# Seven block products in place of eight in part of an MLP's second projection, with a fourth place for split weights

## The chip, the cores and the metric

The kernel runs on one core of a Trainium2 chip. A core has five engines with queues of their own: TensorE (PE) multiplies matrices, VectorE (DVE) and ScalarE (ACT) work elementwise, GpSimd (POOL) does a little here, and SyncE (SP) issues nearly all transfers (DMAs). Operands of the engines lie in an on-chip memory of 128 partitions; products accumulate in eight banks of PSUM, each 128 x 512 float32. The metric is the device time of one execution in microseconds, as the median of several runs.

## What is computed

The reference is one layer of a hybrid encoder over 256 tokens of 2048 features: a mixer with two branches, cross-attention, an MLP and a final norm. The change lies in the MLP:

```python
h = rms_norm(x, norm_ffn_g[l])
x = x + jnp.square(jax.nn.relu(h @ w_ff1[l])) @ w_ff2[l]
return rms_norm(x, norm_final_g)
```

`w_ff1` is 2048 x 8192 and `w_ff2` 8192 x 2048, float32. The hidden activations are 256 x 8192.

## The kernel before

**Split operands.** Each float32 operand of a large product is split into a high part (rounded to the type float32r) and a low part (the rest). A product is then three matmuls: high by high, high by low, low by high. For activations the pair is a *quad*, a tile of four 128-feature blocks by 256 tokens with both parts (`new_quad`); `quad_a` deals them from a ring of five. For weights, `fetch` loads a raw block of 1 MB (2048 float32 columns a partition, ring of three places, `raw`) by one DMA on SP's queue (L104), and splits it in two halves of 1024 columns each: ScalarE copies into `whi` (L117), VectorE subtracts into `wlo` (L118). `whi` and `wlo` have a ring of three places, so three halves can be held at a time. Loads and splits have a high priority in the scheduler, which gives the static order of each engine's queue by a planned time line. `latest` remembers the last split and load, `fetched` all loads; `tc.issue_after(ins)` queues what it encloses behind `ins` on that engine, without a wait.

**The MLP's loop.** The 8192 hidden features are worked off in four quarters, `fb` 0 to 3 (L1124 on). In each quarter:

- *First projection*: eight times `blocks`, each for 256 hidden features (one column pair): 16 feature blocks x 2 column blocks x 2 matmuls (L201 of 512 columns, high weights by both parts of the activations; L202 of 256 columns). `evac_h` (L1130) squares the positive part into `hs` and splits it into the quarter's four quads `hid` (L1134, L1135). In quarter 0, `place` moves 32 tokens at a time of the residual from `tr` to the token-major tile `res`.
- *Second projection*: four times `chunk`, for 512 output columns `n` each. A chunk goes through four stages `q` of 512 hidden features (one raw block each): 4 feature blocks x 2 token halves x 3 matmuls of 512 columns (L158, L159, L160). The two token halves accumulate in PSUM tiles `s0` and `s1`, two each (`stream_ps`); there are four more banks `b` (`bank`). At the end `add` (L1145) adds the scaled sum to `res` on VectorE. The last quarter also takes the sum of squares, and the last chunk (`evac_last`) ends the final norm.

The tiles `rt` and `tr` hold the residual by features and its transpose (16 KB a partition each); after the placement they aren't read any more. `gfin` holds the final gains, 8 KB a partition, loaded ahead of the MLP (L1109).

Of the kernel before, what the change touches and what calls it, by code (L numbers as in the profile page):

```python
# [10 lines left out]
F32 = mybir.dt.float32  # L11
F32R = mybir.dt.float32r
# [5 lines left out]
P = 128  # L18
# [34 lines left out]
def trunk(ctx: ExitStack, tc: tile.TileContext, x_f, mem_f, positions, lead_f, small_f, w_in, ret_gn_g, w_out, w_xq,  # L53
# [20 lines left out]


    fetched, steps, latest = [], [], {}

    @contextmanager
    def behind():
# [15 lines left out]
    def fetch(pieces, k, n, cuts=1, hold=None, at=(0, 0)):  # L95

        raw = wp.tile([P, k * n], F32, name="raw", tag="raw", bufs=3)
        rv = raw.rearrange("p (k n) -> p k n", k=k)
        with tc.high_priority(offset=100000):
            for off, ap in pieces:  # L100
                src = ap.rearrange("(k p) n -> p k n", p=P)
                for c in range(cuts):
                    ks = slice(c * k // cuts, (c + 1) * k // cuts)
                    fetched.append(nc.sync.dma_start(rv[:, ks, off:off + ap.shape[1]], src[:, ks, :]).ins)  # L104
            got = []
            for i in range(2):
                if hold:
                    both = hold().both
                    hi, lo = (both[:, a:a + 2, :].rearrange("p a s -> p (a s)") for a in (0, 2))
                else:  # L110
                    hi, lo = (wp.tile([P, k * n // 2 + room], F32R, name=nm, tag=nm, bufs=3)[:, a:a + k * n // 2]
                              for nm, a, room in zip(("whi", "wlo"), at, (64, 0)))
                src = raw[:, i * k * n // 2:(i + 1) * k * n // 2]
                part = k * n // max(cuts, 2)
                for c in range(0, k * n // 2, part):
                    cs = slice(c, c + part)
                    latest["hi"] = act.activation(hi[:, cs], src[:, cs], AF.Copy).ins  # L117
                    latest["lo"] = vec.tensor_sub(lo[:, cs], src[:, cs], hi[:, cs].bitcast(F32)).ins  # L118
                got.append((hi.rearrange("p (k n) -> p k n", n=n), lo.rearrange("p (k n) -> p k n", n=n)))
            latest["raw"] = fetched[-1]  # L120
        return got
# [23 lines left out]
    def chunk(quads, pieces_of, evac, before=None, hold=None, cuts=1):  # L145

        ps = stream_ps()
        parts = [(t, 0, 512, ps[t]) for t in range(NT)]
        if hold:
            parts[1:] = [(1, 0, 256, ps[1][:, :256]), (1, 256, 512, bank()[:, :256])]  # L150
        held = {q: fetch(pieces_of(q), 4, 512, hold=hold) for q in ((2, 3) if hold else ())}

        def products(q, i, part, halves):
            t, c0, c1, o = part
            xh, xl = (a[:, i, t * P:(t + 1) * P] for a in quads[q])
            wh, wl = (a[:, i % 2, c0:c1] for a in halves[i // 2])
            first, last = q == 0 and i == 0, q == 3 and i == 3
            pe.matmul(o, xh, wh, start=first, stop=False)  # L158
            pe.matmul(o, xh, wl, start=False, stop=False)  # L159
            pe.matmul(o, xl, wh, start=False, stop=last)  # L160

        for q in range(4):
            if q not in held:
                if before and q:
                    before(q)
                halves = fetch(pieces_of(q), 4, 512, cuts=1 if q else cuts)
                if before and not q:
                    before(q)
                for i in range(4):
                    for part in parts:  # L170
                        products(q, i, part, halves)
                    if i % 2:
                        step()
        for part in parts:
            for q, halves in held.items():
                for i in range(4):
                    products(q, i, part, halves)
            with tc.high_priority(offset=50000):
                evac(part[0], part[3], part[1], part[2])
# [93 lines left out]
    def square_sum(acc, src):  # L273
        junk = sm.tile([P, 512], F32, name="junk", tag="junk", bufs=1)
        act.activation(junk[:, :src.shape[1]], src, AF.Square, accum_out=acc)
# [829 lines left out]


    fp = ctx.enter_context(tc.tile_pool(name="mlp", bufs=2))
    gfin = fp.tile([P, D], F32, name="gfin", tag="gfin", bufs=1)
    nc.sync.dma_start(gfin, norm_final_g.partition_broadcast(P))  # L1109
    res = fp.tile([P, NT, D], F32, name="res", tag="res", bufs=1)  # L1110

    tr = fp.tile([P, KT, S], F32, name="tr", tag="tr", bufs=1)
# [3 lines left out]
    def place(b8):  # L1116

        with tc.issue_after(fetched[-1]):
            for a in range(4):
                to = res[b8 % 4 * 32:b8 % 4 * 32 + 32, b8 // 4, :].rearrange("i (k a f) -> i k a f", a=4, f=32)[:, :, a, :]  # L1120
                nc.sync.dma_start(to, tr[32 * a:32 * a + 32, :, b8 * 32:b8 * 32 + 32])

    ssq4 = cp.tile([P, NT, 5], F32, name="ssq4")
    for fb in range(4):  # L1124
        hid = []
        for b2 in range(8):
            hs = fp.tile([P, 2, S], F32, name="hs", tag="hs", bufs=2)
            if b2 % 2 == 0:
                hid.append(quad_a())

            def evac_h(b, ps):
                vec.scalar_tensor_tensor(hs[:, b, :], ps, 0.0, ps, op0=ALU.max, op1=ALU.mult)  # L1132
                qh, ql = (a[:, b2 % 2 * 2 + b, :] for a in hid[-1])
                act.activation(qh, hs[:, b, :], AF.Copy)  # L1134
                vec.tensor_sub(ql, hs[:, b, :], qh.bitcast(F32))  # L1135

            blocks(h3, w_ff1[0], fb * D + b2 * 256, 2, evac_h)
            if fb == 0:
                place(b2)
        for n in range(4):  # L1140
            ns = slice(n * 512, (n + 1) * 512)

            def add(t, ps, c0, c1):
                got = res[:, t, n * 512 + c0:n * 512 + c1]
                vec.scalar_tensor_tensor(got, ps, rstd3q[:, t:t + 1], got, op0=ALU.mult, op1=ALU.add)  # L1145
                return got

            def evac_o(t, ps, c0, c1):
                got = add(t, ps, 0, 512)
                if fb == 3:  # L1150
                    square_sum(ssq4[:, t, n:n + 1], got)
                    vec.tensor_mul(got, got, gfin[:, ns])

            def evac_last(t, ps, c0, c1):
                got = add(t, ps, c0, c1)
                acc = ssq4[:, t, 4 if c0 else 3:5 if c0 else 4]
                if t == 0:
                    square_sum(acc, got)
                else:
                    junk = sm.tile([P, 512], F32, name="junk", tag="junk", bufs=1)  # L1160
                    vec.scalar_tensor_tensor(junk[:, :256], got, 1.0, got, op0=ALU.mult, op1=ALU.mult, accum_out=acc)
                if not c0:
                    s = sm.tile([P, 1], F32, name="s4", tag="s4")
                    vec.tensor_reduce(s, ssq4[:, t, 0:4], axis=AX.X, op=ALU.add)
                    vec.tensor_scalar(s, s, 1.0 / D, EPS, op0=ALU.mult, op1=ALU.add)
                    sums.append(s)
                else:
                    vec.scalar_tensor_tensor(sums[t], acc, 1.0 / D, sums[t], op0=ALU.mult, op1=ALU.add)
                if c1 < 512:
                    return  # L1170
                r = sm.tile([P, 1], F32, name="r4", tag="r4")
                rsqrt(r, sums[t])
                if t == 0:
                    vec.tensor_mul(res[:, t, ns], res[:, t, ns], gfin[:, ns])
                for c in (0, 3, 1, 2):
                    cs = slice(c * 512, (c + 1) * 512)
                    o = res[:, t, cs]
                    if t and c == 3:
                        vec.scalar_tensor_tensor(o, o, r, gfin[:, cs], op0=ALU.mult, op1=ALU.mult)
                    elif t and c == 2:  # L1180
                        vec.tensor_scalar(o, o, r, None, op0=ALU.mult)
                    else:
                        act.activation(o, o, AF.Copy, scale=r)
                    (act if t and c in (3, 2) else nc.sync).dma_start(out[0, t * P:(t + 1) * P, cs], o)

            last = fb == 3 and n == 3
            sums = []
            chunk(hid, cols(w_ff2[0, fb * D:(fb + 1) * D, :], n * 512), evac_last if last else evac_o,
                  hold=quad_b if last else None)


_INS = ["positions", "w_in", "ret_gn_g", "w_out", "w_xq", "w_xkv", "w_xo", "w_ff1", "w_ff2", "norm_final_g"]
# [39 lines left out]
```

## Time and profile before

| what | us |
|---|---|
| median of three runs | 2066.09 (2065.47 to 2066.57) |
| the profiled execution | 2067.12 |
| its span, first to last instruction | 2065.4 |
| TensorE busy | 2055.6 |
| VectorE busy | 1413.0 |
| ScalarE busy | 1097.3 |
| GpSimd busy | 37.4 |

The profile is one execution. Each engine's busy time is the union of its instructions; a matmul's own duration overlaps with the next matmul's, so a pace is read from windows between two events. A group line gives line, engine, operation, tiles, shapes and count, then busy time and mean ns of one, then the idle time before them and what ended it. In timeline rows stand start, duration, engine, line and tiles, and in brackets the idle time before it with its releaser. A row of waits gives who waited for whom: total, times and longest.

### The profile page before, as it was taken

How to read it: one execution, taken by the hardware profiler on the slowest of the kernel's cores; microseconds unless marked ns; L12 is line 12 of the kernel's file. 1: busy time of each engine (PE TensorE's matmuls, PEld its weight loads, DVE VectorE, ACT ScalarE, POOL GpSimd, SP SyncE). 2: the span in 40 equal slices, each digit the busy share in tenths (PEclk: the TensorE clock that was granted, in tenths of full speed). 3: DMA queues.
4: the chain of work that ended last, by engine and by line, in shares of the span. 5: the costliest groups of instructions: out<-in, count | busy, mean ns of one | idle time of the engine just before them, and what ended most of it. 6: DMA issues, size and time to landing. Idle time of an engine off the chain costs nothing.

```text
span 2065.4 us, 28349 instructions
## 1 busy us (share of the span) xinstructions
PE 2055.6 (100%) x10922; PEld 1771.1 (86%) x10922; DVE 1413.0 (68%) x2249; ACT 1097.3 (53%) x1787; POOL 37.4 (2%) x50
## 2 busy tenths in 40 slices
PE   9999999999999999999999999999999999999998
PEld 7888888988888888888888898888888888888887
DVE  5887788779667975887567666776556556655655
ACT  5655764575457455655455555554344434434444
POOL 0000000000000000000000000000000000000000
PEclk9999999999999999999999999999999999999999
DMA  8689556566555655565567654688566566566654
GB/s 323 202 252 302 184 182 198 157 188 201 176 179 186 187 186 173 174 193 182 168 216 233 186 183 142 202 213 222 200 187 194 190 194 193 186 202 185 195 190 143
DMA packets 329224, 405.24 MB, mean 196 GB/s; under 512 B 34928, under 2 KB 239360, under 8 KB 328960
## 3 DMA queue, kind: packets, MB, share of 16 engines
q1 hardware_dynamic: 328656, 402.74, 62.5%
q8 instruction: 85, 1.39, 0.3%
q10 hardware_dynamic: 432, 0.69, 0.1%
q14 instruction: 51, 0.42, 0.1%
HBM read 389.74 MB, written 11.55 MB: 194 GB/s over the span
## 4 chain that ended last, share of the span: by engine, by line
PE 98%; DVE 1%; DMA 0%; issue 0%; ACT 0%; SPq 0%; POOLq 0%; POOL 0%; DVEq 0%; ACTq 0%
PE s L201 33%; PE s L202 17%; PE s L159 13%; PE s L158 13%; PE s L160 13%; PE s L390 1%; PE s L391 1%; PE s L392 1%; PE b L785 1%; PE b L818 1%; PE b L130 0%; PE b L129 0%; PE b L688 0%; PE b L131 0%; PE b L690 0%
## 5 line engine op out<-in xcount | busy, mean ns | idle before, releaser
L118 DVE TENSOR_TENSOR wlo<-raw,whi 128x1024 fp32r<-128x1024 f32 x696 | 851.1, 1223 | 492.2 <-ACT whi L117 486.2
L117 ACT ACTIVATE whi<-raw 128x1024 fp32r<-128x1024 f32 x696 | 737.7, 1060 | 698.9 <-PE s L160 348.6
L201 PE MATMUL s<-q,whi 128*128 128x512 f32 x3072 | 1059.2, 391 | 0.3 <-DVE q L126 0.3
L202 PE MATMUL s<-q,wlo 128*128 128x256 f32 x3072 | 836.8, 281 | 0.2 <-DVE wlo L118 0.2
L201 PEld LDWEIGHTS s<-q,whi 128*128 128x128 f32 x3072 | 566.8, 188 | 111.5 <-DVE q L126 0.5
L202 PEld LDWEIGHTS s<-q,wlo 128*128 128x128 f32 x3072 | 576.9, 188 | 14.2 <-DVE wlo L118 0.6
L159 PE MATMUL s<-wlo,q 128*128 128x512 f32 (+1 forms) x1200 | 469.8, 391 | 0.0
L160 PE MATMUL s<-whi,q 128*128 128x512 f32 (+1 forms) x1200 | 467.4, 390 | 0.0
L158 PE MATMUL s<-whi,q 128*128 128x512 f32 (+1 forms) x1200 | 428.0, 390 | 0.0
L158 PEld LDWEIGHTS s<-whi,q 128*128 128x128 f32 x1200 | 225.2, 188 | 46.9
L160 PEld LDWEIGHTS s<-whi,q 128*128 128x128 f32 x1200 | 225.5, 188 | 45.7
L159 PEld LDWEIGHTS s<-wlo,q 128*128 128x128 f32 x1200 | 225.4, 188 | 45.3
L209 ACT ACTIVATE bo<-s 128x256 f32<-128x256 f32 x192 | 73.2, 381 | 113.0 <-PE s L202 112.9
L210 DVE TENSOR_TENSOR bo<-bo,s 128x256 f32<-128x256 f32 x192 | 80.1, 417 | 55.1 <-ACT bo L209 54.8
L647 DVE SCALAR_TENSOR_TENSOR acc<-bo,small,acc 128x255 f32<-128x255 f32 (+1 forms) x144 | 65.3, 479 | 1.8 <-ACT acc L644 0.6
L754 DVE TENSOR_TENSOR pr<-lw,tw 32x31 f32<-32x31 f32 (+15 forms) x124 | 40.4, 326 | 8.9 <-DMA lw<-scr_l 6.9
L756 DVE TENSOR_TENSOR tw<-tw,pr 32x31 f32<-32x31 f32 (+15 forms) x124 | 40.6, 327 | 2.1
L1145 DVE SCALAR_TENSOR_TENSOR res<-s,rstd3q,res 128x512 f32<-128x512 f32 (+1 forms) x32 | 22.3, 736 | 11.6 <-PE s L160 11.6
L644 ACT ACTIVATE acc<-bo,small 128x256 f32<-128x256 f32 x48 | 24.6, 513 | 7.7 <-DVE bo L210 7.6
L919 ACT ACTIVATE gth<-s 128x512 f32<-128x512 f32 x32 | 18.9, 590 | 17.7 <-PE s L160 12.6
L1132 DVE SCALAR_TENSOR_TENSOR hs<-bo 128x256 f32<-128x256 f32 x64 | 27.0, 423 | 1.1
L1135 DVE TENSOR_TENSOR q<-hs,q 128x256 fp32r<-128x256 f32 x64 | 26.7, 418 | 0.0
(309 smaller groups left out, 1185.0 us busy)
## 6 DMA issues: line engine op xcount, KB each, us to landing
raw<-w_in SPq DMA_DIRECT2D x143, 1024.0 KB
raw<-w_ff SPq DMA_DIRECT2D x128, 1024.0 KB
raw<-w_xkv SPq DMA_DIRECT2D x29, 1024.0 KB
raw<-w_out SPq DMA_DIRECT2D x16, 1024.0 KB
raw<-w_xq SPq DMA_DIRECT2D x16, 1024.0 KB
raw<-w_xo SPq DMA_DIRECT2D x16, 1024.0 KB
dec_d<-dec_w SPq DMA_DIRECT2D x8, 384.0 KB
dec<-dec_d SPq DMA_DIRECT2D x8, 384.0 KB
```

Of the source, the lines that this page charges most:

```text
L117: latest["hi"] = act.activation(hi[:, cs], src[:, cs], AF.Copy).ins
L118: latest["lo"] = vec.tensor_sub(lo[:, cs], src[:, cs], hi[:, cs].bitcast(F32)).ins
L158: pe.matmul(o, xh, wh, start=first, stop=False)
L159: pe.matmul(o, xh, wl, start=False, stop=False)
L160: pe.matmul(o, xl, wh, start=False, stop=last)
L201: pe.matmul(ps[b], lh, xhl, start=kk == 0, stop=False)
L202: pe.matmul(ps[b][:, :S], ll, xh, start=False, stop=kk == KT - 1)
L209: act.activation(o, ps[b][:, S:], AF.Copy)
L210: vec.tensor_add(o, o, ps[b][:, :S])
L647: vec.scalar_tensor_tensor(acc[:, d:], ps[:, :S - d], cw[:, j, blk:blk + 1], acc[:, d:], op0=ALU.mult, op1=ALU.add)
L754: vec.tensor_mul(pv, lw[:, j, j + 1:32].unsqueeze(2).to_broadcast([32, n, j + 1]), tw[:, j, 0:j + 1].unsqueeze(1).to_broadcast([32, n, j + ...
L756: vec.tensor_sub(tw[:, j + 1:32, 0:j + 1], tw[:, j + 1:32, 0:j + 1], pv)
```

## The change

In quarters 0 to 2 the second projection is done by `with_seven` in place of four chunks; quarter 3 stays as it was. Let half of the quarter's hidden features (those of `hid[0]` and `hid[1]`) and columns 0 to 1023 be cut into 2 x 2 blocks: tokens in two halves of 128, hidden features in two sets of 512 (even and odd 128-blocks), columns in two blocks of 512. The 2 x 2 x 2 = 8 block products are replaced by seven products of sums and differences (Winograd's form of Strassen's method), of 4 x 3 matmuls each. The other hidden features of these columns, and all of columns 1024 to 2047, go through plain stages (`plain`) of 24 matmuls as before: 12 of them.

- `token_sums` forms four sums and differences of the hidden activations on VectorE in the first four column pairs of a quarter's first projection, and splits them into `s_hl`.
- `load_block` loads the four weight blocks into `b11`, `b12` (in `rt`) and `b22`, `b21` (in `tr`), each behind the load issued last on SP. `form` subtracts two of them in place, half by half on VectorE, for four of the seven products, and splits the result.
- `issue_after(ends[-1])` keeps all matmuls of a stage behind the stage written before it.
- The partial products go to two banks, `shared` and `p5`, or into the accumulation of the plain stages (`own`). There are 14 additions to `res` in place of 8. Column blocks 3 and 2 use the same two banks one after the other.
- `half_tiles` gives a fourth place for split weights: every fourth half goes to `whx` and `wlx`, in the whole MLP.
- `gfin` lies in `b11` and is loaded after the first projection of quarter 3.

```diff
+    spare, turn = [], [0]
+    def half_tiles():
+        turn[0] += 1
+        if spare and turn[0] % 4 == 0:
+            return tuple(spare[0].tile([P, 1024 + room], F32R, name=nm, tag=nm, bufs=1)
+                         for nm, room in (("whx", 128), ("wlx", 0)))
+        return tuple(wp.tile([P, 1024 + room], F32R, name=nm, tag=nm, bufs=3) for nm, room in (("whi", 64), ("wlo", 0)))
...
-                    hi, lo = (wp.tile([P, k * n // 2 + room], F32R, name=nm, tag=nm, bufs=3)[:, a:a + k * n // 2]
-                              for nm, a, room in zip(("whi", "wlo"), at, (64, 0)))
+                    hi, lo = (h[:, a:a + k * n // 2] for h, a in zip(half_tiles(), at))
...
-    gfin = fp.tile([P, D], F32, name="gfin", tag="gfin", bufs=1)
-    nc.sync.dma_start(gfin, norm_final_g.partition_broadcast(P))
...
+    s_hl = tuple(fp.tile([P, 4, 512], F32R, name="s" + e, tag="s" + e, bufs=1) for e in "hl")
+    b11, b12, b22, b21 = (a[:, c:c + 8, :].rearrange("p k s -> p (k s)") for a in (rt, tr) for c in (0, 8))
+    gfin = b11
+    spare.append(fp)
+    def add(n, t, ps, c0=0, c1=512):
+        got = res[:, t, n * 512 + c0:n * 512 + c1]
+        with tc.high_priority(offset=50000):
+            vec.scalar_tensor_tensor(got, ps, rstd3q[:, t:t + 1], got, op0=ALU.mult, op1=ALU.add)
+        return got
+    def token_sums(i, hs):
+        sv = fp.tile([P, 4, P], F32, name="sv", tag="sv", bufs=1)
+        (a11, a21), (a12, a22) = ((hs[:, b, 0:P], hs[:, b, P:S]) for b in range(2))
+        vec.tensor_add(sv[:, 0], a21, a22)
+        vec.tensor_sub(sv[:, 1], sv[:, 0], a11)
+        vec.tensor_sub(sv[:, 2], a11, a21)
+        vec.tensor_sub(sv[:, 3], a12, sv[:, 1])
+        split([a[:, i, :] for a in s_hl], sv.rearrange("p a s -> p (a s)"))
+    def with_seven(hid, rows):
+        own = [stream_ps() for _ in range(2)]
+        shared, p5 = bank(), bank()
+        own += [[bank(), bank()]] * 2
+        opened, ends = set(), []
+        def load_block(to, which, n):
+            src = rows[0:D // 2, n * 512:(n + 1) * 512].rearrange("(i two p) n -> p i two n", two=2, p=P)[:, :, which, :]
+            with tc.issue_after(fetched[-1]), tc.high_priority(offset=100000):
+                fetched.append(nc.sync.dma_start(to.rearrange("p (i n) -> p i n", i=4), src).ins)
+        def triple(o, lhs, rhs, key, last=False):
+            for j, (l, r) in enumerate(((0, 0), (0, 1), (1, 0))):
+                with tc.issue_after(ends[-1]) if ends else ExitStack():
+                    ins = pe.matmul(o, lhs[l], rhs[r], start=key not in opened, stop=last and j == 2,
+                                    skip_group_check=True).ins
+                opened.add(key)
+            return ins
+        def plain(n, q):
+            halves = fetch(cols(rows, n * 512)(q), 4, 512)
+            for i in range(4):
+                for t in range(NT):
+                    ins = triple(own[n][t], [a[:, i, t * P:(t + 1) * P] for a in hid[q]],
+                                 [a[:, i % 2, :] for a in halves[i // 2]], (n, t), q == 3 and i == 3)
+            ends.append(ins)
+        def form(raw, minus=None):
+            got = []
+            with tc.high_priority(offset=100000):
+                for c in range(2):
+                    cs = slice(c * 1024, (c + 1) * 1024)
+                    if minus:
+                        with tc.issue_after(latest["lo"]):
+                            vec.tensor_sub(raw[:, cs], *(a[:, cs] for a in minus))
+                    hi, lo = (h[:, :1024] for h in half_tiles())
+                    latest["hi"] = act.activation(hi, raw[:, cs], AF.Copy).ins
+                    latest["lo"] = vec.tensor_sub(lo, raw[:, cs], hi.bitcast(F32)).ins
...
+        plain(3, 0)
+        load_block(b11, 0, 0)
+        plain(3, 1)
+        load_block(b12, 0, 1)
+        product(shared, part(0, 0), form(b11), "shared")
+        add(0, 0, shared)
+        plain(3, 2)
+        load_block(b22, 1, 1)
+        product(p5, summed(0), form(b11, (b12, b11)), "p5")
+        add(1, 0, p5)
+        add(1, 1, p5)
+        plain(0, 2)
+        product(own[1][0], summed(3), form(b22), (1, 0))
+        plain(3, 3)
+        load_block(b21, 1, 0)
+        for t in range(NT):
+            add(3, t, own[3][t])
+        product(shared, summed(1), form(b11, (b22, b11)), "shared")
+        add(1, 0, shared)
+        plain(0, 3)
+        product(own[0][0], part(1, 0), form(b21), (0, 0))
+        add(0, 0, own[0][0])
+        plain(2, 0)
+        product(shared, summed(2), form(b12, (b22, b12)), "shared")
+        add(0, 1, shared)
+        add(1, 1, shared)
+        plain(1, 2)
+        plain(2, 1)
+        product(own[0][1], part(1, 1), form(b11, (b21, b11)), (0, 1))
+        add(0, 1, own[0][1])
+        plain(2, 2)
+        plain(2, 3)
+        for t in range(NT):
+            add(2, t, own[2][t])
+        plain(1, 3)
+        for t in range(NT):
+            add(1, t, own[1][t])
...
+                if fb < 3 and b2 < 4 and b:
+                    token_sums(b2, hs)
...
+        if fb < 3:
+            with_seven(hid, rows)
+            continue
+        with tc.issue_after(fetched[-1]):
+            nc.sync.dma_start(gfin, norm_final_g.partition_broadcast(P))
```

More of the change, by code (lines that the diff above doesn't have):

```diff
@@ new lines, in token_sums, with product, part, summed @@
+    def token_sums(i, hs):
[40 more added lines that the diff above has]
+                    latest["lo"] = vec.tensor_sub(lo, raw[:, cs], hi.bitcast(F32)).ins
+                    got.append((hi.rearrange("p (k n) -> p k n", n=512), lo.rearrange("p (k n) -> p k n", n=512)))
+            return got
+        def product(o, lhs, halves, key):
+            for i in range(4):
+                ins = triple(o, lhs(i), [a[:, i % 2, :] for a in halves[i // 2]], key, i == 3)
+            ends.append(ins)
+        def part(b, t):
+            return lambda i: [a[:, 2 * (i % 2) + b, t * P:(t + 1) * P] for a in hid[i // 2]]
+        def summed(j):
+            return lambda i: [a[:, i, j * P:(j + 1) * P] for a in s_hl]
+        plain(3, 0)
[35 more added lines that the diff above has]
+            add(1, t, own[1][t])
@@ L1124, in trunk @@
     for fb in range(4):
         hid = []
+        rows = w_ff2[0, fb * D:(fb + 1) * D, :]
         for b2 in range(8):
@@ L1139, in trunk @@
                 place(b2)
+        if fb < 3:
[3 more added lines that the diff above has]
+            nc.sync.dma_start(gfin, norm_final_g.partition_broadcast(P))
         for n in range(4):
             ns = slice(n * 512, (n + 1) * 512)
[L1143 to L1146, printed above, removed]
             def evac_o(t, ps, c0, c1):
[L1149 to L1152, printed above, removed]
+                got = add(n, t, ps)
+                square_sum(ssq4[:, t, n:n + 1], got)
+                vec.tensor_mul(got, got, gfin[:, ns])
             def evac_last(t, ps, c0, c1):
-                got = add(t, ps, c0, c1)
+                got = add(n, t, ps, c0, c1)
                 acc = ssq4[:, t, 4 if c0 else 3:5 if c0 else 4]
@@ L1184, in evac_last @@
                     (act if t and c in (3, 2) else nc.sync).dma_start(out[0, t * P:(t + 1) * P, cs], o)
-            last = fb == 3 and n == 3
+            last = n == 3
             sums = []
-            chunk(hid, cols(w_ff2[0, fb * D:(fb + 1) * D, :], n * 512), evac_last if last else evac_o,
-                  hold=quad_b if last else None)
+            chunk(hid, cols(rows, n * 512), evac_last if last else evac_o, hold=quad_b if last else None)
 _INS = ["positions", "w_in", "ret_gn_g", "w_out", "w_xq", "w_xkv", "w_xo", "w_ff1", "w_ff2", "norm_final_g"]
```

## The prediction

> **What bounds the kernel now.** I read the page first: the share of busy time, its slices, the granted clock, the chain that ended last, and the groups that the change touches.
>
> ```profile
> PE 2055.6 (100%) x10922; PEld 1771.1 (86%) x10922; DVE 1413.0 (68%) x2249; ACT 1097.3 (53%) x1787; POOL 37.4 (2%) x50
> ...
> PE   9999999999999999999999999999999999999998
> ...
> PEclk9999999999999999999999999999999999999999
> ...
> PE 98%; DVE 1%; DMA 0%; issue 0%; ACT 0%; SPq 0%; POOLq 0%; POOL 0%; DVEq 0%; ACTq 0%
> ...
> L118 DVE TENSOR_TENSOR wlo<-raw,whi 128x1024 fp32r<-128x1024 f32 x696 | 851.1, 1223 | 492.2 <-ACT whi L117 486.2
> L117 ACT ACTIVATE whi<-raw 128x1024 fp32r<-128x1024 f32 x696 | 737.7, 1060 | 698.9 <-PE s L160 348.6
> ...
> L159 PE MATMUL s<-wlo,q 128*128 128x512 f32 (+1 forms) x1200 | 469.8, 391 | 0.0
> ...
> L1145 DVE SCALAR_TENSOR_TENSOR res<-s,rstd3q,res 128x512 f32<-128x512 f32 (+1 forms) x32 | 22.3, 736 | 11.6 <-PE s L160 11.6
> ```
>
> TensorE works through the whole span at the full granted clock, and 98% of the chain is TensorE's. The next view lists everything TensorE waited for.
>
> ```profile
> PE b L248 <- DVE warm L244: 1.1, 1, 1.1
> PE s L390 <- DVE q L325: 0.6, 1, 0.6
> PE s L201 <- DVE q L126: 0.3, 1, 0.3
> PE s L202 <- DVE wlo L118: 0.2, 1, 0.2
> ```
>
> Four waits, 2.2 us together, none of them in the MLP. So a matmul that goes away shortens the end by its full price, and any new wait of TensorE lengthens it by its full length. There is no idle time here to be won besides.
>
> The price of a matmul isn't the 391 ns of its group, since matmuls overlap. The windows view gives the pace. I cut it at the first additions to `res`, which follow the ends of the chunks, then over the four chunks of the first quarter.
>
> ```profile
> core 0: us, PE busy (x) PEld busy (x) DVE busy (x) ACT busy (x) POOL busy (x), PEclk, DMA share, GB/s
> 1465.24:1487.00 21.76, 21.76 (x97) 18.02 (x97) 11.12 (x12) 8.49 (x8) 0.00 (x0) 1.00 0.58 194
> ...
> 1443.48:1530.52 87.04, 87.04 (x386) 72.11 (x385) 45.29 (x45) 35.11 (x36) 0.00 (x0) 1.00 0.60 194
> ```
>
> A chunk of 96 matmuls takes 21.76 us, so a 512-column matmul costs 226.7 ns of path. The second projection of a quarter takes 87.04 us, in which VectorE is busy for 45.29 and ScalarE for 35.11.
>
> **The change, part by part.** *Removed: 12 matmuls in each of three quarters.* One block product is 4 x 3 = 12 matmuls. Seven in place of eight make 12 plain stages x 24 + 7 x 12 = 372, where 4 x 96 = 384 stood. 12 x 226.7 ns = 2.72 us a quarter, **8.16 us** for three: 372 then take 84.3 us. The Trainium skill, page "TensorE: Matmul & The Clock Gate", Part 1, gives N / 2.4 GHz + 2.5 ns between starts, 215.7 ns at 512 columns; by that figure 36 matmuls would be worth 7.8 us. The measured pace is the longer one, and I keep it.
>
> *Added: forming the blocks.* Weights of 1 MB are split in two halves, each by one ScalarE copy (L117) and one VectorE subtraction (L118). Before, a quarter has 16 such blocks, 32 halves. After, 12 plain stages and 7 products make 19 blocks, 38 halves; four products first subtract two weight blocks, two instructions of 1024 columns each. This subtraction, all operands f32, isn't in the trace. The nearest rows are L118 (1.22 us, same size) and the transpose below (1.21 us, f32 to f32). I take 1.22; 1.1 and 1.4 would be bounds, below zero it can't go.
>
> ```profile
> L1114 DVE STREAM_TRANSPOSE tr<-rt 128x1024 f32<-128x1024 f32 x4 | 4.6, 1213 | 0.0
> ```
>
> VectorE in the seven-product stage: 38 x 1.22 + 8 x 1.22 + 14 additions (for 8) x 0.74 = 46.4 + 9.8 + 10.4 = 66.6 us of 84.3. ScalarE: 38 x 1.06 = 40.3. Both fit as sums, 79% and 48%. What decides is whether each half is ready when TensorE asks for it, so I follow one in the order of time (a timeline of one half).
>
> ```profile
> 1454.64 0.62 PE L158 MATMUL s<-whi,q 128*128 128x512 f32 x2
> 1454.84 1.06 ACT L117 ACTIVATE whi<-raw 128x1024 fp32r<-128x1024 f32 x1 [1.60 <-PE s L160]
> ...
> 1455.94 1.23 DVE L118 TENSOR_TENSOR wlo<-raw,whi 128x1024 fp32r<-128x1024 f32 x1 [1.44 <-ACT whi L117]
> ...
> 1457.36 0.62 PE L158 MATMUL s<-whi,q 128*128 128x512 f32 x2
> ```
>
> A half lasts TensorE 2.72 us in a plain stage (1454.64 to 1457.36), so 1.36 in a product. When TensorE leaves a half, its place is refilled: the copy starts 0.20 us after the next half's first matmul, the subtraction 1.10 after the copy, and takes 1.23. A refilled place is ready 2.53 us after it came free. With three places that is 2.9 us ahead of need, with four 5.6.
>
> Now a product whose block is a difference. Let T be the time at which TensorE starts it; before it come a product and a plain stage. The plain stage's last half takes the place freed four halves earlier, at T - 2 x 1.36 - 2 x 2.72 = T - 8.16, and is ready at T - 5.63. Behind it on VectorE stands the first weight subtraction, to T - 4.4; copy to T - 3.3; split to T - 2.0. The first half is 2 us early. The second subtraction may only follow that split: to T - 0.8; copy to T + 0.3; split to T + 1.56. TensorE reads this low part from its second matmul on, T + 1.36 + 0.23 = T + 1.59. It just fits. The halves behind it catch up within 11 us, and the fourth difference has two plain stages ahead of it and 2.7 us more. So the walk gives no stall from the differences themselves.
>
> One of them has a neighbour, though. Just ahead of the second difference (the fourth product, `shared` with `summed(1)`) TensorE ends column block 3, and its two additions come due at T + 0.2, while VectorE waits for the copy until T + 0.3.
>
> ```profile
> 1465.24 1.40 DVE L1145 SCALAR_TENSOR_TENSOR res<-s,rstd3q,res 128x512 f32<-128x512 f32 x2
> ```
>
> Two take 1.40 us. If neither goes first the stall is 0; if one does, the split ends at about T + 2.1, 0.5 late; if both do, 1.24 late. I take one: 0.5 us a quarter, **1.5 us** in all, with 0 and 3.7 as ends. What is queued behind the split on VectorE is the next stage's first low half, which the walk has ready 0.2 us before TensorE's need, and the addition left over, for which nothing waits soon.
>
> *Added: sums of tokens*, in four of the eight column pairs of the first projection: four 128 x 128 operations, and one split of 512 columns.
>
> ```profile
> L890 DVE TENSOR_TENSOR st<-b,dm 128x128 f32<-128x128 f32 x8 | 2.2, 280 | 0.0
> ...
> L125 ACT ACTIVATE q<-xn 128x512 fp32r<-128x512 f32 x8 | 4.7, 624 | 0.2 <-DVE xn L495 0.2
> L1152 DVE TENSOR_TENSOR res<-res,gfin 128x512 f32<-128x512 f32 x6 | 3.9, 685 | 0.0
> ```
>
> ```profile
> 1542.00:1553.00 11.00, 11.00 (x66) 9.74 (x65) 7.09 (x10) 5.36 (x9) 0.00 (x0) 1.00 0.64 191
> ```
>
> That is 4 x 0.28 + 0.69 = 1.8 us of VectorE, and at most 0.62 of waiting for the copy. VectorE idles 3.9 of 11.0 us in such a pair and the refills stand 5.6 us ahead, so I cost it at nothing. Without that cover it would be 2.4 us x 12 pairs, 29 us.
>
> *Transfers.* The number of 1 MB loads stays at 16 a quarter; four now have places of their own and are issued behind a stage's load on SP. `gfin` (1 MB) moves from ahead of the MLP into its last quarter.
>
> ```profile
> SPq L104 <- DVE wlo L118: 912.4, 199, 9.6
> ```
>
> ```profile
> L1109 SPq DMA_DIRECT2D gfin<-norm_final_g x1: 340/340/340, 1364.6 to 1364.6; - x1
> ```
>
> SP's loads wait for a free place, not for the DMA engines, which are 0.60 busy at 194 GB/s (the window above): 1.05 MB take about 3.3 us alone. The second difference operand is loaded 13 us before its use, `gfin` 21.8 us before its first reader. Cost 0; with no cover, 3.3 us for each load that is late.
>
> *Order.* TensorE keeps the written stage order. Inside a stage nothing changes; the re-used PSUM banks (`shared`, and column block 2 in the bank of 3) are re-entered two or more stages after their additions, 8 us at least. Cost 0.
>
> **Sum.** -8.16 + 1.5 = -6.7 us. The profiled execution took 2067.12 us (span 2065.4), 1.0 above the median of the three runs, 2066.09; its own sum is 2060.5, and against the median **2059.4 us**.
>
> **The rivals.** *First, slower: the lead is three places' worth, not four.* Everything hangs on 0.03 us of margin in the second half. If one instruction of a split's length stands in front of the weight subtraction, or the fourth place is refilled a product half (1.36 us) later, each of three differences comes 1.33 us late, and the additions behind them still cost 0.5 to 1.24: 4.5 to 5.2 us a quarter, 13.5 to 15.7 in all, against 8.16. That is 2071.4 to 2073.6, slower. It decides from 2.72 us of stall a quarter upward. For it: the wait of L118 for L117 is already VectorE's largest (486 us), and it stands in a difference's chain twice. The skill's page on TensorE, Part 1, "Architectural detail", says that ScalarE and VectorE are strict first-in-first-out, which would make any such order final; no row here shows a queue overtaken. Against it: the walk counted no overlap between neighbouring VectorE instructions.
>
> *Second, the gain is halved or gone: a slower pace or partial stalls.* The pace isn't the same everywhere. The first output projection has the same pairs of matmuls as the second.
>
> ```profile
> 1096.14 0.42 DVE L1011 TENSOR_TENSOR rt<-bo,xc 128x256 f32<-128x256 f32 x1
> 1107.43 0.43 DVE L1011 TENSOR_TENSOR rt<-bo,xc 128x256 f32<-128x256 f32 x1
> 1311.35 0.42 DVE L1011 TENSOR_TENSOR rt<-bo,rt 128x256 f32<-128x256 f32 x1
> 1322.38 0.43 DVE L1011 TENSOR_TENSOR rt<-bo,rt 128x256 f32<-128x256 f32 x1
> ```
>
> One pair of columns took 11.29 us there and 11.03 here, 2.4% more, and no view says why. If the 372 matmuls ran at such a pace, 84.3 x 0.024 x 3 = 6.1 us would be lost: 2064.0 without stalls. Stalls of 1.4 to 4.1 us a quarter give 2062.0 to 2070.2. Against it: all MLP chunks of before keep the one pace.
>
> *Third, all of it: no stall at all,* additions last. 2057.9.
>
> **How the numbers follow.** About 0.2%, 4.1 us, is what a measurement of this kernel can tell from no change. The forecast, with stalls above 0 and up to 1.4 us a quarter (2058.0 to 2062.0), has 0.45; the third case 0.17; the second rival, which lies within 0.2% of before, 0.20; the first 0.18. Forecast and third case together give the likeliest sign its own range, 2057.6 to 2062.0. The subtraction's bounds (1.1 to 1.4) move the second half by -0.2 to +0.4 us, 3 us over nine differences, inside these cases. The range reaches from 2057.6 through nearly all of the second rival, 2069; the first is left out. Faster 0.62, same 0.20, slower 0.18.
>
> **What would show it.** 36 fewer matmuls (10886); 84.3 us plus stalls between the end of a quarter's first projection and the next quarter's start; VectorE at 66 to 67 us in it. New rows in TensorE's waits, for the second half's low part in the products of differences, some 0.5 us in the fourth product and next to none elsewhere, show the walk right. Waits above 1 us in three products a quarter mean the first rival; a pace above 227 ns without waits the second. Waits at column pairs of the first projection would show that the token sums aren't covered, waits for a DMA that the loads aren't: then the prediction is wrong at a place where I costed nothing.

## The result, and the profile after

The changed kernel takes **2061.46 us** (median of 17 runs, 2059.37 to 2063.12), the kernel before 2065.52 beside it (17 runs, 2063.89 to 2066.92): a ratio of 0.998 with a 95% interval of 0.9972 to 0.9987. It is faster by 4.1 us. The prediction had 6.7 and 2059.4; the time lies inside its range.

The page of the profile after (execution 2061.57 us):

```profile
span 2059.9 us, 28433 instructions
...
PE 2047.6 (99%) x10886; PEld 1761.5 (86%) x10886; DVE 1487.2 (72%) x2369; ACT 1119.7 (54%) x1817; POOL 36.4 (2%) x50
...
PE   9999999999999999999999999999999999999998
...
PEclk9999999999999999999999999999999999999999
...
PE 98%; DVE 1%; issue 0%; ACT 0%; DMA 0%; SPq 0%; POOLq 0%; POOL 0%; ACTq 0%
```

There are 36 matmuls fewer, as counted, and 120 more VectorE instructions; TensorE still sets the end. What is new is in the view of TensorE's waits, cut to the MLP, which was empty before:

```profile
PE b L1168 <- DVE wlx L1191: 1.0, 1, 1.0
PE b L1168 <- DVE wlo L1191: 0.8, 2, 0.4
PE s L209 <- DVE bo L218: 0.6, 1, 0.6
```

The first two rows are three waits of a block product (L1168) for a low half of a weight difference (L1191), one a quarter. The third is one wait of the first projection in quarter 0. The windows view, cut where the stages end, prices them. Its columns are the stretch and its length, then busy time and count of each engine, the granted clock, the DMA engines' share and GB/s.

```profile
1443.23:1528.69 85.46, 85.07 (x374) 69.59 (x373) 64.80 (x65) 39.96 (x42) 0.00 (x0) 1.00 0.51 168
1528.69:1616.87 88.18, 88.18 (x513) 78.16 (x513) 61.42 (x96) 44.50 (x66) 0.00 (x0) 1.00 0.72 228
1616.87:1702.66 85.79, 84.84 (x374) 69.58 (x373) 64.95 (x65) 41.10 (x42) 0.00 (x0) 1.00 0.48 158
1790.84:1876.26 85.42, 85.03 (x374) 69.59 (x373) 64.80 (x65) 39.94 (x42) 0.00 (x0) 1.00 0.48 159
1361.95:1443.23 81.28, 80.70 (x461) 70.33 (x461) 61.00 (x98) 40.84 (x63) 0.70 (x1) 1.00 0.99 256
```

The second projections take 85.46, 85.79 and 85.42 us, where quarters 0 to 2 of before took 87.07, 87.07 and 87.08 by the same cut. Without a wait 372 matmuls take 84.35 (both subtractions first, below), so 1.1, 1.4 and 1.1 us are lost, 3.6 in all, and the three stages gain 4.55 us. The wait rows name only 1.8 of these 3.6. A wait counts from the end of the matmul in flight (0.39 us after its start), while the path loses from the next start that the pace of 0.227 would have given, and the next matmul after a wait starts 0.34 us behind it in place of 0.227. Another 0.8 us lie in the first and third differences, whose second half is ready only just in time: there the matmul behind it starts 0.28 to 0.34 us later in place of 0.227, and no wait row appears. **A stage's length tells the cost; the wait rows tell the place.**

The first projections of quarters 1 to 3 take 88.18 us each (before, 88.30). That of quarter 0 takes 81.28 (last row) where before takes 79.47 by the same cut: 0.65 of the 1.8 us come with the wait, as the experiments below show. The other 1.15 come with a slower pace of matmuls from 1398 us on (last section).

The two profiles differ by 5.5 us in span. 2.5 of these lie ahead of the MLP, where the matmuls stand in the same order in both kernels: the MLP starts at 1361.6 us instead of 1364.1. That is run against run and not the change. The MLP's own sum, without the slower pace, is -4.55 - 0.35 + 0.65 = -4.25 us, next to the measured -4.1.

### The profile page after: what moved, and what is told of

It reads as the page before. It is cut to its first block, busy times and chain, and to the rows that moved or that the text cites. A ratio compares the mean times of both kernels' runs of the same rounds, so it can differ in the third digit from the quotient of the medians.

```text
span 2059.9 us, 28433 instructions
## 1 busy us (share of the span) xinstructions
PE 2047.6 (99%) x10886; PEld 1761.5 (86%) x10886; DVE 1487.2 (72%) x2369; ACT 1119.7 (54%) x1817; POOL 36.4 (2%) x50
## 4 chain that ended last, share of the span: by engine, by line
PE 98%; DVE 1%; issue 0%; ACT 0%; DMA 0%; SPq 0%; POOLq 0%; POOL 0%; ACTq 0%
PE s L209 34%; PE s L210 18%; PE s L167 9%; PE s L166 9%; PE s L168 9%; PE b L1168 7%; PE s L1168 4%; PE s L398 1%; PE s L400 1%; PE s L399 1%; PE b L793 1%; PE b L696 1%; PE b L826 1%; PE b L138 0%; PE b L137 0%; PE b L139 0%
## 5 line engine op out<-in xcount | busy, mean ns | idle before, releaser
L126 DVE TENSOR_TENSOR wlo<-raw,whi 128x1024 fp32r<-128x1024 f32 x613 | 748.8, 1222 | 354.6 <-ACT whi L125 348.1
L209 PE MATMUL s<-q,whi 128*128 128x512 f32 x2816 | 974.1, 391 | 0.8 <-DVE bo L218 0.6
L125 ACT ACTIVATE whi<-raw 128x1024 fp32r<-128x1024 f32 x613 | 649.2, 1060 | 556.8 <-PE s L209 211.3
L167 PE MATMUL s<-wlo,q 128*128 128x512 f32 x788 | 309.7, 393 | 0.0
L168 PE MATMUL s<-whi,q 128*128 128x512 f32 x788 | 307.3, 390 | 0.0
L166 PE MATMUL s<-whi,q 128*128 128x512 f32 x788 | 286.7, 390 | 0.0
L166 PEld LDWEIGHTS s<-whi,q 128*128 128x128 f32 x788 | 147.8, 188 | 30.9
L168 PEld LDWEIGHTS s<-whi,q 128*128 128x128 f32 x788 | 148.1, 188 | 29.7
L167 PEld LDWEIGHTS s<-wlo,q 128*128 128x128 f32 x788 | 148.1, 188 | 29.5
L126 DVE TENSOR_TENSOR wlx<-raw,whx 128x1024 fp32r<-128x1024 f32 x59 | 72.2, 1223 | 37.2 <-ACT whx L125 36.3
L1168 PE MATMUL b<-whi,q 128*128 128x512 f32 x300 | 95.7, 389 | 0.0
L209 PE MATMUL s<-q,whx 128*128 128x512 f32 x256 | 89.7, 390 | 0.0
L1168 PEld LDWEIGHTS b<-whi,q 128*128 128x128 f32 x300 | 56.3, 188 | 11.8
L1168 PE MATMUL b<-wlo,q 128*128 128x512 f32 x150 | 58.4, 389 | 0.0
```

The source lines that it names most:

```text
L209: pe.matmul(ps[b], lh, xhl, start=kk == 0, stop=False)
L1168: ins = pe.matmul(o, lhs[l], rhs[r], start=key not in opened, stop=last and j == 2, skip_group_check=True).ins
```

## The experiments

**The theory** is the prediction's walk: what TensorE loses is the lateness of the second half of a difference, set by the chain subtraction, copy, split on VectorE, by how many places ahead the splits may run, and by the additions that stand in VectorE's queue ahead of the last split. **The rivals**: the loss is in the pace or in the first projection; or it comes from late weight loads or the refill of places, whatever VectorE's order is. All times below are medians of runs beside the kernel before on the same chip (2065.98 us for the first four, 2066.17 for the last four).

VectorE's timeline in the changed kernel shows the chain at the fourth product:

```profile
1475.36 1.23 DVE L1191 TENSOR_TENSOR wlo<-rt,whi 128x1024 fp32r<-128x1024 f32 x1 [1.21 <-ACT whi L1190]
1476.50 1.22 DVE L1188 TENSOR_TENSOR rt<-tr,rt 128x1024 f32<-128x1024 f32 x1
1478.18 1.43 DVE L1138 SCALAR_TENSOR_TENSOR res<-b,rstd3q,res 128x512 f32<-128x512 f32 x2 [0.46 <-PE b L1168]
1479.53 1.22 DVE L1191 TENSOR_TENSOR wlo<-rt,whi 128x1024 fp32r<-128x1024 f32 x1
```

After the second subtraction (L1188) VectorE waits for TensorE to end column block 3, does *both* additions (1.43 us), and only then splits (1479.53 to 1480.75). TensorE's timeline answers to it; the first row is the start of the product, the prediction's T:

```profile
1478.66 0.39 PE L1168 MATMUL b<-whi,sh 128*128 128x512 f32 x1
...
1480.02 0.39 PE L1168 MATMUL b<-whi,sh 128*128 128x512 f32 x1
1480.80 0.50 PE L1168 MATMUL b<-wlo,sh 128*128 128x512 f32 x1 [0.39 <-DVE wlo L1191]
```

The first addition starts at 1478.18, 0.48 us before T, since the bank of one token half is finished before that of the other. So the pair ends at T + 0.95, and TensorE's read comes 0.55 us after its due time, T + 1.59. Quarter 2 repeats this. In quarter 1 a split of the next stage (L126) has gone ahead of the two additions as well, and the read is 1.1 us late:

```profile
1650.04 1.22 DVE L1188 TENSOR_TENSOR rt<-tr,rt 128x1024 f32<-128x1024 f32 x1
1651.17 1.22 DVE L126 TENSOR_TENSOR wlo<-raw,whi 128x1024 fp32r<-128x1024 f32 x1
1652.31 1.40 DVE L1138 SCALAR_TENSOR_TENSOR res<-b,rstd3q,res 128x512 f32<-128x512 f32 x2
1653.63 1.22 DVE L1191 TENSOR_TENSOR wlx<-rt,whx 128x1024 fp32r<-128x1024 f32 x1
```

### Three places

```diff
-    spare.append(fp)
```

> The changed kernel without the fourth place for split weights: three places, as before. If TensorE's waits come from the chain subtraction, copy, split on VectorE and from the lead of the places (the prediction's walk), each of the first three differences is now over 1 us late and the additions still stand ahead of the second: 3.5 to 5 us of waits a quarter where the profile of the changed kernel shows 1.1 to 1.5, so the second projection of quarters 0 to 2 takes 88 to 89 us each where it takes 85.4 to 85.8, and the time is 2068 to 2072 us, at or above the kernel before. If instead what is lost lies in the pace of matmuls or in the first projection, the stages stay at 85.4 to 85.8 us and the time stays within 1 us of the changed kernel.

It took **2071.99 us**, ratio 1.0029 [1.0019, 1.0039]: slower than before. The second projections take 88.9 us each. In the MLP TensorE waits nine times for the low half of a difference, three times a quarter:

```profile
PE b L1167 <- DVE wlo L1190: 6.9, 9, 0.8
PE b L1167 <- ACT whi L1189: 0.6, 3, 0.2
```

88.9 - 84.35 = 4.6 us a quarter. That is the first rival's sum in the prediction (4.5 to 5.2), and its time (2071.4 to 2073.6), but not quite its parts: each of the three differences loses 1.5 us (1.33 forecast), the second no more than the others, so the additions cost nothing of their own here (0.5 to 1.24 forecast). They run while VectorE would wait for the copy anyway:

```profile
1478.80 1.22 DVE L1187 TENSOR_TENSOR rt<-tr,rt 128x1024 f32<-128x1024 f32 x1
1479.93 1.40 DVE L1137 SCALAR_TENSOR_TENSOR res<-b,rstd3q,res 128x512 f32<-128x512 f32 x2
1481.25 1.22 DVE L1190 TENSOR_TENSOR wlo<-rt,whi 128x1024 fp32r<-128x1024 f32 x1
```

The lead of the splits is what decides in this form of the code; the pace isn't.

### The additions behind the split

```diff
-        for t in range(NT):
-            add(3, t, own[3][t])
-        product(shared, summed(1), form(b11, (b22, b11)), "shared")
+        second = form(b11, (b22, b11))
+        with tc.issue_after(latest["lo"]):
+            for t in range(NT):
+                add(3, t, own[3][t])
+        product(shared, summed(1), second, "shared")
```

> The two additions of column block 3 are queued on VectorE behind the split of the second difference. The walk: this product's wait (0.9 to 1.3 us a quarter) shrinks below 0.2 us, the stages take 84.4 to 84.8 us, the time falls by 2 to 3 us against the changed kernel, to about 2059. If the additions have nothing to do with it (the chain of the difference alone is late, or the pace is slow), the wait stays and the time with it, 2061 to 2062.

It took **2062.10 us**, ratio 0.9979 [0.997, 0.9988]: no gain over the changed kernel, so the expectation missed. The wait at the difference is gone in all quarters, but two new ones stand one stage later, at a plain stage's low half:

```profile
PE s L1168 <- DVE wlo L126: 1.1, 2, 0.6
```

```profile
1478.87 1.23 DVE L1191 TENSOR_TENSOR wlo<-rt,whi 128x1024 fp32r<-128x1024 f32 x1 [1.21 <-ACT whi L1190]
1480.01 1.40 DVE L1138 SCALAR_TENSOR_TENSOR res<-b,rstd3q,res 128x512 f32<-128x512 f32 x2
1481.33 1.21 DVE L126 TENSOR_TENSOR wlo<-raw,whi 128x1024 fp32r<-128x1024 f32 x1
```

The split now comes first (1478.87), the additions next, and the next stage's first split is pushed back behind them. The walk had given that half 0.2 us to spare, and an addition pair takes 1.40. In quarter 1 the queue happens to hold another split in between, and its stage is 84.49 us; the others are 85.64 and 85.75. The three stages together are 0.8 us shorter than in the changed kernel's profile, which the median doesn't show. The additions add to the wait at the difference, as the theory had it, but in quarters 0 and 2 moving them only moves the wait: in this order VectorE's queue has no room for them before the next stage's split.

### Both subtractions first

```diff
                 for c in range(2):
-                    cs = slice(c * 1024, (c + 1) * 1024)
-                    if minus:
-                        with tc.issue_after(latest["lo"]):
-                            vec.tensor_sub(raw[:, cs], *(a[:, cs] for a in minus))
+                cuts = [slice(c * 1024, (c + 1) * 1024) for c in range(2)]
+                if minus:
+                    with tc.issue_after(latest["lo"]):
+                        for cs in cuts:
+                            vec.tensor_sub(raw[:, cs], *(a[:, cs] for a in minus))
+                for cs in cuts:
                     hi, lo = (h[:, :1024] for h in half_tiles())
```

> Both halves of a weight subtraction come ahead of the first half's copy and split, so the second half's copy needn't wait for the first half's split: by the walk the second half is ready 2.4 us sooner, ahead of the additions too. All waits at differences vanish, stages of 84.3 to 84.5 us, the time 3 to 3.5 us below the changed kernel, about 2058. If the waits came from late weight loads or the refill of places, nothing changes: 2061 to 2062.

It took **2058.00 us**, ratio 0.9961 [0.9949, 0.9974]. No wait for a difference is left, and the stages are as long as their matmuls:

```profile
1441.95:1526.30 84.35, 84.35 (x373) 69.82 (x373) 64.86 (x65) 40.84 (x42) 0.00 (x0) 1.00 0.53 178
```

```profile
1471.45 2.35 DVE L1188 TENSOR_TENSOR rt<-tr,rt 128x1024 f32<-128x1024 f32 x2
1473.88 2.36 DVE L1192 TENSOR_TENSOR wlo<-rt,whi 128x1024 fp32r<-128x1024 f32 x2
1476.15 1.22 DVE L126 TENSOR_TENSOR wlo<-raw,whi 128x1024 fp32r<-128x1024 f32 x1
1477.29 1.40 DVE L1138 SCALAR_TENSOR_TENSOR res<-b,rstd3q,res 128x512 f32<-128x512 f32 x2
```

The same VectorE work (64.86 us of 84.35) runs without the idle stretches, up to 1.21 us each, in which VectorE waited for the copies of a difference: the second subtraction fills the first copy's time. The loads and the places are as they were, so the rival that blames them falls.

### The fourth place alone

The kernel before with `half_tiles` and `spare.append(fp)`, nothing else.

> The kernel before with the fourth place alone. TensorE has no wait in the MLP before, so the walk expects no change: within 1 us of the kernel before, and each second projection 87.0 us. If the fourth place by itself costs something in quarter 0's first projection (81.3 us in the changed kernel's profile where before has 79.5, part of it a wait of 0.6 us at 1372 us and part a slower pace from 1398 us on), it shows here too, as 0.6 to 1.8 us.

It took **2066.91 us**, ratio 1.0005 [0.9996, 1.0014]: no difference from before that the interval shows. But the wait of quarter 0's first projection is there, and it is the only one that the view shows in the MLP:

```profile
PE s L209 <- DVE bo L218: 0.6, 1, 0.6
```

```profile
1364.73 4.62 DVE L1122 STREAM_TRANSPOSE tr<-rt 128x1024 f32<-128x1024 f32 x4
1369.27 1.18 DVE L126 TENSOR_TENSOR wlx<-raw,whx 128x1024 fp32r<-128x1024 f32 x1
```

The split for the fourth place stands behind VectorE's four transposes, 4.6 us late. In the static order the scheduler has TensorE do three parts of the next column pair meanwhile, so the first pair ends late, and the third pair waits for its PSUM bank to be read. The price is 0.65 us, once. This profile loses another 0.35 us at 1400 us, where a low half comes just too late: its copy on ScalarE had waited 4.55 us for the load. In every profile with the fourth place from the start ScalarE waits 3.5 to 4.6 us for a load there, in none of the others over 2.5. On the other side, all later first projections are 0.12 us shorter with a fourth place (88.18 for 88.30), in every profile, though no wait goes away; why stays open. That gives about half of the 0.65 back.

### The fourth place from the second pair on

Both subtractions first, and:

```diff
-    spare.append(fp)
...
                 place(b2)
+                if b2 == 1:
+                    spare.append(fp)
```

> Both subtractions first, and the fourth place handed out only after the second column pair of quarter 0. In every profile with the fourth place from the start TensorE waits 0.6 us at the third column pair of quarter 0 for a PSUM read (L218), in none without. If that comes from the fourth place's first split standing behind VectorE's four transposes, the wait goes, quarter 0's first projection takes 79.8 to 79.9 us instead of 80.5, the stages stay at 84.35, and the time is 0.6 us below the version with the subtractions first, about 2057.4. If it comes from the token sums or from the missing gfin load, the wait stays.

It took **2057.01 us** (2056.67 to 2057.42), ratio 0.9958 [0.9946, 0.9971]. Quarter 0's first projection, counted from the norm's matmuls on as in the expectation, takes 79.78 us and has no wait (before: 79.83): the fourth place's first split was the cause, not the sums nor the load. It has the lowest median of all versions, 9.2 us below the kernel before on the same chip, but its interval overlaps those of the other versions with both subtractions first: the profile shows the 0.6 us, the medians don't.

### Both subtractions first, three places

Both subtractions first, and without `spare.append(fp)`.

> Both subtractions first, without the fourth place. The walk, with every refill 1.36 us later: first half ready at T - 0.6, second at T + 0.6 where it is needed at T + 1.6; so no wait at the differences themselves, and 0 to 0.3 us at the stage behind the second, where the additions stand ahead of a split. Stages of 84.4 to 84.8 us, no wait in quarter 0's first projection, the others 88.3 us: 2057.5 to 2059, so the fourth place would be needless. If a lead of four places is needed whatever the order of the subtractions, stages of 86 us or more and 2062 us or more.

It took **2058.79 us**, ratio 0.9966 [0.9953, 0.9978], without one wait in the MLP:

```profile
1443.83:1528.18 84.35, 84.35 (x374) 69.82 (x373) 65.12 (x65) 41.19 (x42) 0.00 (x0) 1.00 0.50 168
```

So the fourth place is needed only because of the order inside `form`. With the subtractions in front, three do for the products.

### Token sums once

```diff
-                if fb < 3 and b2 < 4 and b:
+                if fb < 1 and b2 < 4 and b:
```

> Both subtractions first, fourth place kept; leaves out the token sums of quarters 1 and 2, whose products use those of quarter 0. The prediction costs the sums at nothing: the first projections of quarters 1 and 2 stay at 88.18 us and all else too. If they cost, these two get shorter by more than 0.1 us each.

The first projections of quarters 1 and 2 take 88.18 us, with the sums and without:

```profile
1526.81:1614.99 88.18, 88.18 (x514) 78.17 (x513) 55.45 (x76) 42.42 (x62) 0.00 (x0) 1.00 0.71 228
```

VectorE has 6 us less to do there (55.45 for 61.42), and nobody waits for it. The single time was 2057.47 us, of a kernel that leaves these sums out. With three places the cover isn't quite whole: in both profiles with three places and the sums, the first projections of quarters 1 and 2 take 88.34 to 88.35 us, and that of quarter 3, which has no sums, 88.29.

### No written order

```diff
-                with tc.issue_after(ends[-1]) if ends else ExitStack():
-                    ins = pe.matmul(...)
+                ins = pe.matmul(...)
```

> Both subtractions first, fourth place kept, and no written order for TensorE's stages: the scheduler orders the matmuls by its planned time line. If the written order is what keeps the loads of split weights spread (a plain stage between two products), stages mix and waits or a slower pace return: 2059 to 2063. If it only fixes what the planner would do anyway, the stages stay at 84.4 us and the time at 2058.

It took **2057.46 us** (2055.73 to 2060.03), ratio 0.9958 [0.9944, 0.9971], with stages of 84.37, 84.35 and 84.35 us. The planner moves a few matmuls across the borders of stages, and that changes nothing: once no half is late, the written order costs and brings nothing in these stages. The profile has one more wait of 0.4 us, in quarter 0's first projection, at a low half behind a load, as at 1400 us with the fourth place alone:

```profile
PE s L210 <- DVE wlo L126: 0.4, 1, 0.4
```

Whether the order matters where halves are late wasn't tried.

## Why the prediction was right, and where it was off

- *TensorE bounds, and a matmul is worth its pace:* right. 36 matmuls fewer, and stages of 84.35 us once nothing waits; 87.07 - 84.35 is 2.72 a quarter, the predicted figure: the pace of before held. By the 215.7 ns of the Trainium skill's page "TensorE: Matmul & The Clock Gate", Part 1, it would be an estimated 2.59; the measured pace decides.
- *The walk of a difference:* right in its mechanism. With the additions aside it had 0.03 us to spare for the second half; the first and third difference lost 0.1 to 0.2 us each, the second the most, and the fourth, with two plain stages ahead, nothing. The weight subtraction took 1.22 us, the value taken. VectorE's sum was too high (64.8 to 65.0 us measured for 66 to 67), since neighbouring instructions overlap: the rows above start 1.14 us apart and last 1.22.
- *The additions,* "I take one": **this is the term that was mis-sized.** Both went ahead in all three quarters (in one with another split besides), and the second difference lost 0.7, 1.2 and 0.7 us where 0.5 stood; the end that the prediction gave for both was 1.24. That the wait in quarters 0 and 2 is as late as the 0.5 for *one* addition is luck: two ran, but the first began 0.48 us before T and not 0.2 after it. With the losses at the first and third difference, put at next to nothing, the stalls are 3.6 us for 1.5 predicted, near their upper end of 3.7.
- *The next stage's half with 0.2 us to spare:* right, and it mattered more than the text made of it. It is why putting the additions behind the split gained nothing. The Trainium skill's page "TensorE: Matmul & The Clock Gate" (Part 1, "Architectural detail") calls VectorE "strict FIFO". The trace agrees: the wait moved to the split that stands next in VectorE's queue (1481.33, behind the additions' 1.40 us).
- *Token sums, transfers, order at nothing:* right, but for 0.06 us a quarter of the sums with three places. The sums were tried, and the free order too; TensorE has no wait for the loads of the blocks. The prediction's sign for uncovered sums, a wait at a column pair of the first projection, did appear, but it belongs to the fourth place.
- *The fourth place* was costed only as a lead. That its first split would stand behind the transposes and cost 0.65 us once wasn't seen; 0.35 us of shorter first projections make up for about half of it. Stalls of 3.6 for 1.5 and these 0.3 us are the 2.4 us between the forecast gain of 6.7 and the 4.25 that the profile accounts for.
- *The first rival* (slower) has the time of the kernel with three places. Its cause, the missing lead, is right; its split between lead and additions isn't (1.5 us at each difference and nothing for the additions), so that the sum fits is partly luck. *The third* (no stall at all, 2057.9) describes the kernel with the subtractions first.

## What to carry to other kernels

Where a product trades matmuls for elementwise work on the operands, the sum of that work says little (76 and 77% of the stage here, with and without waits); walk the chain of one operand against the moment at which TensorE needs it, with every instruction that can stand ahead of it in its queue. A chain that goes back and forth between two engines is shortened by issuing the first engine's next piece before it waits for the second: that did more here than one more buffer, which it made needless. And when a wait is removed by moving work, look one stage further before counting the gain.

## What the runs showed of the hardware

The same matmuls have more than one pace. In the first output projection, whose matmuls stand in the same order in before and after, 40 us hold 229 matmuls in the profile of before and 234 in that of after:

```profile
1100.00:1140.00 40.00, 40.00 (x229) 34.76 (x228) 27.32 (x41) 20.88 (x33) 0.00 (x0) 1.00 0.68 211
```

```profile
1100.00:1140.00 40.00, 40.00 (x234) 35.42 (x233) 27.53 (x43) 22.44 (x36) 0.00 (x0) 1.00 0.69 209
```

From start to start, a 512-column matmul followed by one of 256 columns takes 236 ns there in the one and 226.7 in the other, at the same granted clock. The slow pace holds without a break for tens of microseconds; in this projection it costs 1.4 us, of the 2.5 us ahead of the MLP by which the two profiles differ. In this place it was there in the profiles of before and of six experiments, and not in three (after; both subtractions first; sums once). In the changed kernel's profile quarter 0's first projection has a stretch of it from 1398 to 1443 us, which costs 1.15 us. A third pace, 230 ns, holds in this stretch in the profiles of the sums once and of the free order. The two rows above show the same clock, and about the same transfer rate and share. It may be part of why runs of one kernel differ by 3 us; the prediction's second rival had it as a possible cost of the change. What sets the pace stays open.
